# Cumulated gates carried by the scores' second matmul, causal mask read by VectorE from one constant tile

## The chip, the cores and the metric

The kernel runs on one core of a Trainium2 chip. The metric is device time in microseconds (us) of one execution. The engines of a core are PE (TensorE, matrix products), DVE (VectorE), ACT (ScalarE), POOL (GpSimd) and SP (SyncE, which here only issues DMAs). Each engine works through its own instruction list in order, and they meet at semaphores.

## What is computed

One decoder layer on a sequence of 1024 positions of width 1024, in float32. Two groups of heads read the same modulated input; eight of them are the forgetting-attention ("fox") heads that this change is about:

```python
cum = cumsum(log_f)                        # one running sum per head, over the positions
s = einsum('qd,kd->qk', q, k) * scale      # head width 64, scale 1/8
s = s + cum[q] - cum[k]
s = where(key_pos <= q_pos, s, -inf)       # causal mask
p = softmax(s); out = p @ v
```

`cum[q]` is the same for a whole row of scores, so the softmax doesn't see it and the kernel leaves it out. Around the fox heads stand a conditioning row, an input projection, four retention heads, an output projection with a norm, and a gated MLP with a width-3 convolution and a second norm.

## The kernel before

Matrices are split into a high part in fp32r and the rest (`whi`/`wlo`, `hhi`/`hlo`), and a product is made of three matmuls. The program has two parts. A first block `r` (input modulation, retention heads, and the projection `vp` of the fox values and gates) is ordered by a scheduler's simulation. The rest follows it: attention, output projection, MLP.

*Start.* SP loads the conditioning vector `cs` and its bias `bcol`, then, for each of eight slices j of the model width, two slices of modulation weights (`ada`), one of input weights (`wrr`) and one of the transposed input (`xt`). DVE makes scale and shift from `ada`, ACT makes `hhi` from `xt`, and PE runs 21 matmuls per slice (`fa`, `fb`). Before that PE runs matmuls on a tile `warm` of ones.

*End of block r.* `v_proj(c, n)` runs 24 matmuls for each of 16 steps q. `log_forget` makes the log gates `L`, `cum_forget` sums them on PE (`pcum`), `cum_store` turns the result (`pcumT`), copies it (`cumT`) and stores it in DRAM as `cum_d`.

*Attention.* It runs in 64 steps, eight query blocks i for each of eight heads h. `fox_proj(h, .., t, part)` projects queries and keys of half t of the sequence, in four parts of six matmuls, and in its last part ACT and DVE split the result: `qh` holds the high part of -q/8 twice (rows 0-63 and 64-127), `ql` the low part twice, `ks` the high part of k over its low part. `fox_scores(h, i)` multiplies `qh` by `ks` (L799) and `ql` by `ks` (L800), which adds the four products of the parts; a third matmul (L803) multiplies the bf16 identity `identb` by `maskb` and so adds 1e30 above the diagonal of the last 128 columns. DVE (L805) then adds the tile `nb`, the head's cumulated gates broadcast to 128 rows by a DMA of 512 KB, and takes the row minimum in the same instruction; ACT (L812) takes the exponential, POOL (L816) divides. Three steps later `fox_turn` transposes the block on PE (`pt`, L866), ACT (L874) and DVE (L875) split it, and `fox_pv` multiplies by the values. `fox_w(h)` loads and splits the weights of head h as a whole into a pair of tiles of its own, one head ahead.

*Passengers of the attention stage.* `park_load`, `park_high` (ACT, L1032), `park_low` (DVE) and `park_store` split the output weights in 16 loads that pass through SBUF tiles `park` back into DRAM (`wod`), two or three per head; `park_high` of the first load stands on ACT between the exponentials of steps 1 and 2. `down_base(m)` issues on SP, in step 6 of head m, its share of 44 copies of 256 KB from the down-projection weights into a DRAM tensor `td`, which the MLP reads much later. These copies are kept behind the head's `nb` load:

```python
def fox_alloc(h):
    ...
    pins["nb"] = nc.sync.dma_start(t["nb"], ...)
def down_base(m):
    ...
        with tc.issue_after(pins["nb"].ins):
            nc.sync.dma_start(td[q, k], wdq[t, k][:, n * 512:(n + 1) * 512])
```

`issue_after(x)` gives the instructions inside it a place behind x in the list of x's engine; it reaches only instructions on that engine. Instructions with no such edge and no data to wait for are placed wherever the ordering pass finds room. SP's DMAs report on eight semaphores in turn, and a DMA is issued only when the one that last used its semaphore has landed, so at most eight are under way.

The functions that the change touches, with the profile's line numbers:

Of the kernel before, what the change touches and what calls it, by code (L numbers as in the profile page):

```python
# [31 lines left out]
def kernel(  # L32
# [43 lines left out]
    def f(ap):  # L76
        return ap.bitcast(F32)
# [4 lines left out]
    identb = cp.tile([P, P], BF16, tag="identb", name="identb")  # L82
    nc.vector.tensor_copy(identb, ident)
# [4 lines left out]
    maskb = cp.tile([P, P], BF16, tag="maskb", name="maskb")  # L88
    nc.gpsimd.memset(maskb, 0.0)
    nc.gpsimd.affine_select(  # L90
        out=maskb, in_=maskb, pattern=[[-1, P]], compare_op=ALU.is_ge,
        fill=BIG, base=0, channel_multiplier=1,
    )
# [542 lines left out]
    def fox_w(h):  # L636
        raw = slot("R", [P, ND, P], F32, f"wqkr{h}")
        nc.sync.dma_start(raw, w_qk[h])
        whi = slot("X", [P, ND, P], F32R, f"wqh{h}")
        wlo = slot("X", [P, ND, P], F32R, f"wql{h}")  # L640
        nc.scalar.copy(whi, raw)
        for q in range(2):
            sl = slice(4 * q, 4 * q + 4)
            nc.vector.tensor_tensor(
                out=wlo[:, sl, :], in0=raw[:, sl, :], in1=f(whi[:, sl, :]), op=ALU.subtract
            )
        return whi, wlo
# [4 lines left out]
    cum_d = dp.tile([64, P], F32, tag="cum_d", name="cum_d")  # L652
# [67 lines left out]
    def cum_store(cum):  # L720
        pc = bank("pcumT")
        turn(pc[:64, :P], cum.rearrange("p c h -> p (c h)"), ident)
        cumT = tmp([64, P], F32, "cumT")
        nc.vector.tensor_copy(cumT, pc[:64, :P])
        nc.sync.dma_start(cum_d, cumT)

    for q in range(2 * NT):
# [7 lines left out]
        if q == 3:  # L735
            w = fox_w(0)
        if q == 8:
            Lp = log_forget()
        if q == 14:
            cum = cum_forget(Lp)  # L740
            nw = fox_w(1)
        if q == 15:
            cum_store(cum)
# [5 lines left out]

    def fox_alloc(h):  # L750
        t = {n: slot("X", [P, S], F32R, f"{n}{h}") for n in ("qh", "ql", "ks")}
        t["nb"] = slot("X" if h < 2 else "VM", [P, S], F32, f"nb{h}")
        pins["nb"] = nc.sync.dma_start(t["nb"], bass.AP(
            tensor=cum_d.tensor, offset=cum_d.offset + h * S, ap=[[0, P], [1, S]]))
        return t

    def fox_proj(h, w, T, t, part):
        whi, wlo = w
# [1031 lines left out]
```

## Time and profile before

| | |
|---|---|
| median of 3 runs | 1214.06 us (1213.79 to 1214.09) |
| profiled execution: time / span | 1213.8 us / 1212.1 us |
| granted TensorE clock | 0.998 of full speed |
| PE busy / DVE / ACT / POOL | 1195.2 / 912.2 / 655.7 / 229.6 us |
| attention, first to last score matmul | 280.7 to 473.8 us |
| moved by DMA | 216.57 MB, mean 179 GB/s |

The span is the profile's own time from first to last event; the execution's time is 1.7 us longer. A group row of the profile gives line, engine, operation, output and inputs, count, busy time and the mean of one. Rows of the timeline begin with start and duration. In rows of windows the DMA share is the mean busy share of the 16 DMA engines (it can come out a little above 1), and GB/s is what they moved. "SPq" rows are DMA issues by SP; the time from issue to landing stands in the rows on DMA issues.

### The profile page before, as it was taken

How to read it: one execution, taken by the hardware profiler on the slowest of the kernel's cores; microseconds unless marked ns; L12 is line 12 of the kernel's file. 1: busy time of each engine (PE TensorE's matmuls, PEld its weight loads, DVE VectorE, ACT ScalarE, POOL GpSimd, SP SyncE). 2: the span in 40 equal slices, each digit the busy share in tenths (PEclk: the TensorE clock that was granted, in tenths of full speed). 3: DMA queues.
4: the chain of work that ended last, by engine and by line, in shares of the span. 5: the costliest groups of instructions: out<-in, count | busy, mean ns of one | idle time of the engine just before them, and what ended most of it. 6: DMA issues, size and time to landing. Idle time of an engine off the chain costs nothing.

```text
span 1212.1 us, 17100 instructions
## 1 busy us (share of the span) xinstructions
PE 1195.2 (99%) x5957; PEld 1000.4 (83%) x5957; DVE 912.2 (75%) x1749; ACT 655.7 (54%) x1209; POOL 229.6 (19%) x274
## 2 busy tenths in 40 slices
PE   8999999999999999999999999999999999999997
PEld 6788888997888888888888888888888888888885
DVE  7847657766888888456988778787787875886686
ACT  6635445346777776567754545454454555644452
POOL 0015345012333333000021322211000010000021
PEclk9999999999999999999999999999999999999999
DMA  9524354605474659223268987776554589975741
GB/s 359 227 87 121 134 158 138 202 34 175 160 239 156 191 162 356 94 79 113 87 181 203 205 210 182 176 180 175 155 139 125 145 238 289 326 247 190 263 175 70
DMA packets 94279, 216.57 MB, mean 179 GB/s; under 512 B 10784, under 2 KB 17136, under 8 KB 94192
## 3 DMA queue, kind: packets, MB, share of 16 engines
q1 hardware_dynamic: 81520, 192.40, 45.7%
q0 software_dynamic: 12672, 23.07, 11.9%
q8 instruction: 47, 0.77, 0.3%
q14 instruction: 40, 0.33, 0.1%
HBM read 173.45 MB, written 76.59 MB: 206 GB/s over the span
## 4 chain that ended last, share of the span: by engine, by line
PE 91%; DMA 4%; DVE 2%; ACT 1%; issue 0%; SPq 0%; DVEq 0%
PE rp L152 11%; PE dX L1531 10%; PE dZ L1531 7%; PE uX L1306 7%; PE uX L1307 7%; PE uX L1305 7%; PE uY L1307 5%; PE uY L1306 5%; PE uY L1305 5%; PE vp L152 4%; PE pv L886 3%; DMA ada<-in_ada_dram 3%; PE op L191 2%; PE op L189 2%; PE op L190 2%; PE pt L866 2%
## 5 line engine op out<-in xcount | busy, mean ns | idle before, releaser
L152 PE MATMUL rp<-wr,hhi 128*128 128x512 f32 x400 | 127.9, 401 | 0.0
L1517 DVE TENSOR_TENSOR dl<-dr,dh 128x1024 fp32r<-128x1024 f32 x66 | 80.5, 1238 | 33.8 <-ACT dh L1505 31.5
L816 POOL TENSOR_TENSOR S<-S,dn 128x128 f32<-128x128 f32 (+3 forms) x64 | 74.2, 1166 | 151.3 <-DVE dn L815 112.0
L1505 ACT CAST dh<-dr 128x1024 fp32r<-128x1024 f32 x58 | 59.8, 1051 | 65.6 <-DMA dr<-td 30.3
L1148 POOL DMA_DIRECT2D sd<-gd x22 | 18.1, 823 | 396.9 <-DMA sd<-y 226.2
L152 PEld LDWEIGHTS rp<-wr,hhi 128*128 128x128 f32 x400 | 71.6, 189 | 12.7
L152 PE MATMUL rp<-wr,hlo 128*128 128x512 f32 x200 | 78.6, 393 | 0.0
L1531 PE MATMUL dX<-dl,dh 128*128 128x512 f32 x176 | 68.5, 389 | 0.0
L1531 PE MATMUL dX<-dh,dl 128*128 128x512 f32 x176 | 68.5, 389 | 0.0
L1531 PE MATMUL dX<-dh 128*128 128x512 f32 x176 | 68.5, 389 | 0.0
L1320 ACT COPY u<-uX 128x512 f32<-128x512 f32 x44 | 25.8, 586 | 70.3 <-PE uX L1307 70.3
L812 ACT ACTIVATE S<-S,mn 128x128 f32<-128x128 f32 (+3 forms) x64 | 49.8, 779 | 23.9 <-DVE mn L805 23.7
L152 DVE CUSTOM_DVE_ANT_0 ada<-ada,csb,bcol 128x1024 f32<-128x1024 f32 x46 | 60.1, 1310 | 3.4 <-DMA ada<-in_ada_dram 3.3
L875 DVE TENSOR_TENSOR pt<-pt,pt 128x384 fp32r<-128x384 f32 (+3 forms) x104 | 51.9, 517 | 10.2 <-ACT pt L874 9.8
L874 ACT CAST pt<-pt 128x384 fp32r<-128x384 f32 (+3 forms) x104 | 45.2, 454 | 24.9 <-PE pt L866 23.5
L765 PE MATMUL qk<-hhi,wqh 128*128 128x512 f32 x128 | 54.3, 424 | 1.8 <-DVE ks L777 1.5
L1531 PE MATMUL dZ<-dh 128*128 128x512 f32 x132 | 51.6, 391 | 0.0
L1531 PE MATMUL dZ<-dl,dh 128*128 128x512 f32 x132 | 51.4, 389 | 0.0
L1531 PE MATMUL dZ<-dh,dl 128*128 128x512 f32 x132 | 51.4, 389 | 0.0
L767 PE MATMUL qk<-hhi,wql 128*128 128x512 f32 x128 | 51.0, 399 | 0.0
L766 PE MATMUL qk<-hlo,wqh 128*128 128x512 f32 x128 | 50.9, 397 | 0.0
L189 PE MATMUL op<-wo,mxs 128*128 128x512 f32 x128 | 50.7, 396 | 0.0
(1049 smaller groups left out, 3653.3 us busy)
## 6 DMA issues: line engine op xcount, KB each, us to landing
ada<-in_ada_dram SPq DMA_DIRECT2D x48, 512.0 KB, 3.9
td<-in_w_down_dram SPq DMA_DIRECT2D x44, 256.0 KB, 5.6
wa<-in_w_up_dram SPq DMA_DIRECT2D x22, 512.0 KB, 4.5
wb<-in_w_up_dram SPq DMA_DIRECT2D x22, 512.0 KB, 3.7
gd<-y SPq DMA_DIRECT2D x22, 512.0 KB, 2.7
sd<-y SPq DMA_DIRECT2D x44, 256.0 KB, 3.1
dr<-sd SPq DMA_DIRECT2D x44, 256.0 KB, 4.2
dr<-td SPq DMA_DIRECT2D x44, 256.0 KB, 4.4
```

Of the source, the lines that this page charges most:

```text
L152: order[key] = fn(*args, **kw)
L189: mm(pt, ahi, whi, start=start, stop=False)
L765: nc.tensor.matmul(pt, whi[:, j, :], hhi[j][:, sl], start=(j == 0), stop=False)
L767: nc.tensor.matmul(pt, wlo[:, j, :], hhi[j][:, sl], start=False, stop=(j == ND - 1))
L816: nc.gpsimd.tensor_tensor(out=Ssb[:, :span], in0=Ssb[:, :span], in1=den.to_broadcast([P, span]), op=ALU.mult,)
L875: nc.vector.tensor_tensor(out=dl, in0=src, in1=f(dh), op=ALU.subtract)
L1305: nc.tensor.matmul(pt, whi, bh, start=start, stop=False, skip_group_check=True)
L1306: nc.tensor.matmul(pt, whi, bl, start=False, stop=False, skip_group_check=True)
L1307: nc.tensor.matmul(pt, wlo, bh, start=False, stop=stop, skip_group_check=True)
L1505: nc.scalar.copy(hi, raw)
L1517: nc.vector.tensor_tensor(out=lo, in0=raw, in1=f(hi), op=ALU.subtract)
L1531: nc.tensor.matmul(pt, w_[:, 0, q], m_[:, 1, :], start=start and n_ == 0, stop=stop and n_ == 2, skip_group_check=True)
```

## The change

- The mask's matmul, its identity and its tile go. A constant tile `late` [128, 1024] (zeros, and 1e30 above the diagonal in its last 128 columns) takes the place of `nb` as DVE's second operand in the row minimum.
- The cumulated gates enter through the second score matmul. `cum_store` splits them into three fp32r parts and stores them as `cum_d` [3, 64, 128]. Per head a DMA on POOL's queue puts three rows of 4 KB into rows 64-66 of a tile `kc`, under the low part of k, and two constant tiles `q1` carry ones in these rows under the high part of q. The first product is now `qq` (high over low q) by `kk` (high k twice), the second `q1` by `kc` with 67 rows.
- `fox_w` works in halves into one pair of tiles for all heads, at steps 1 and 3 of the head before; the load `fox_load` stands at step 4, one head earlier. `cum_forget` and `cum_store` stand two steps of q earlier.
- `pins["nb"]` is now the `kc` DMA on POOL, so `down_base` names an instruction of POOL's list while its copies are on SP's.

```diff
@@ -79,18 +79,10 @@
 
     ident = cp.tile([P, P], F32, tag="ident", name="ident")
     make_identity(nc, ident)
-    identb = cp.tile([P, P], BF16, tag="identb", name="identb")
-    nc.vector.tensor_copy(identb, ident)
     epsc = cp.tile([P, 1], F32, tag="epsc", name="epsc")
     nc.vector.memset(epsc, LN_EPS)
     ones = cp.tile([P, P], F32, tag="ones", name="ones")
     nc.vector.memset(ones, 1.0)
-    maskb = cp.tile([P, P], BF16, tag="maskb", name="maskb")
-    nc.gpsimd.memset(maskb, 0.0)
-    nc.gpsimd.affine_select(
-        out=maskb, in_=maskb, pattern=[[-1, P]], compare_op=ALU.is_ge,
-        fill=BIG, base=0, channel_multiplier=1,
-    )
     tri = cp.tile([P, P], F32, tag="tri", name="tri")
     nc.gpsimd.memset(tri, 1.0)
     nc.gpsimd.affine_select(
@@ -633,23 +625,24 @@
             v_load(2 * (c - 2))
 
 
-    def fox_w(h):
-        raw = slot("R", [P, ND, P], F32, f"wqkr{h}")
-        nc.sync.dma_start(raw, w_qk[h])
-        whi = slot("X", [P, ND, P], F32R, f"wqh{h}")
-        wlo = slot("X", [P, ND, P], F32R, f"wql{h}")
-        nc.scalar.copy(whi, raw)
-        for q in range(2):
-            sl = slice(4 * q, 4 * q + 4)
-            nc.vector.tensor_tensor(
-                out=wlo[:, sl, :], in0=raw[:, sl, :], in1=f(whi[:, sl, :]), op=ALU.subtract
-            )
-        return whi, wlo
+    wraw = {}
+
+    def fox_load(h):
+        wraw[h] = slot("R", [P, ND, P], F32, f"wqkr{h}")
+        nc.sync.dma_start(wraw[h], w_qk[h])
+
+    def fox_w(h, half):
+        sl = slice(4 * half, 4 * half + 4)
+        raw, (whi, wlo) = wraw[h], wqk
+        nc.scalar.copy(whi[:, sl, :], raw[:, sl, :])
+        nc.vector.tensor_tensor(
+            out=wlo[:, sl, :], in0=raw[:, sl, :], in1=f(whi[:, sl, :]), op=ALU.subtract
+        )
 
 
     L = cp.tile([P, NT, FH], F32, tag="L", name="L")
     V2 = [slot("VM", [P, NT, P], F32R, f"V2_{h}") for h in range(FH)]
-    cum_d = dp.tile([64, P], F32, tag="cum_d", name="cum_d")
+    cum_d = dp.tile([3, 64, P], F32, tag="cum_d", name="cum_d")
 
     def v_proj(c, n):
         n0, n1 = (0, 256) if n == 0 else (256, 520)
@@ -720,9 +713,15 @@
     def cum_store(cum):
         pc = bank("pcumT")
         turn(pc[:64, :P], cum.rearrange("p c h -> p (c h)"), ident)
-        cumT = tmp([64, P], F32, "cumT")
-        nc.vector.tensor_copy(cumT, pc[:64, :P])
-        nc.sync.dma_start(cum_d, cumT)
+        parts = tmp([64, 3 * P], F32R, "cumT").rearrange("h (u q) -> h u q", u=3)
+        rest = tmp([64, P], F32, "cumr")
+        nc.vector.tensor_copy(parts[:, 0, :], pc[:64, :P])
+        nc.vector.tensor_tensor(out=rest, in0=pc[:64, :P], in1=f(parts[:, 0, :]),
+                                op=ALU.subtract)
+        nc.vector.tensor_copy(parts[:, 1, :], rest)
+        nc.vector.tensor_tensor(out=parts[:, 2, :], in0=rest, in1=f(parts[:, 1, :]),
+                                op=ALU.subtract)
+        nc.sync.dma_start(cum_d.rearrange("u h q -> h u q"), f(parts))
 
     for q in range(2 * NT):
         n, c = 1 - q // NT, q % NT
@@ -733,30 +732,45 @@
         if q in (2, 10):
             mod_rows(q // 8)
         if q == 3:
-            w = fox_w(0)
+            wqk = [slot("X", [P, ND, P], F32R, f"wq{n}") for n in "hl"]
+            fox_load(0)
+            for half in range(2):
+                fox_w(0, half)
         if q == 8:
             Lp = log_forget()
+        if q == 12:
+            cum = cum_forget(Lp)
+        if q == 13:
+            cum_store(cum)
         if q == 14:
-            cum = cum_forget(Lp)
-            nw = fox_w(1)
-        if q == 15:
-            cum_store(cum)
+            fox_load(1)
 
     blk.__exit__(None, None, None)
 
     mixF = {}
     pins = {}
 
+    late = slot("X", [P, S], F32, "late")
+    nc.gpsimd.memset(late, 0.0)
+    nc.gpsimd.affine_select(
+        out=late[:, S - P:], in_=late[:, S - P:], pattern=[[-1, P]], compare_op=ALU.is_ge,
+        fill=BIG, base=0, channel_multiplier=1,
+    )
+    q1s = [slot("X", [P, S], F32R, f"q1_{p}") for p in range(2)]
+    NC = 64 + 3
+    for q1 in q1s:
+        nc.gpsimd.memset(f(q1[64:NC, :]), 1.0)
+
     def fox_alloc(h):
-        t = {n: slot("X", [P, S], F32R, f"{n}{h}") for n in ("qh", "ql", "ks")}
-        t["nb"] = slot("X" if h < 2 else "VM", [P, S], F32, f"nb{h}")
-        pins["nb"] = nc.sync.dma_start(t["nb"], bass.AP(
-            tensor=cum_d.tensor, offset=cum_d.offset + h * S, ap=[[0, P], [1, S]]))
+        t = {"qq": slot("X", [P, S], F32R, f"qq{h}"), "kk": slot("X", [P, S], F32R, f"kk{h}"),
+             "kc": slot("X" if h < 2 else "VM", [P, S], F32R, f"kc{h}"), "q1": q1s[h % 2]}
+        pins["nb"] = nc.gpsimd.dma_start(
+            t["kc"][64:NC, :].rearrange("u (c q) -> u c q", q=P), cum_d[:, h * NT:h * NT + NT, :])
         return t
 
-    def fox_proj(h, w, T, t, part):
-        whi, wlo = w
-        qh, ql, ks = T["qh"], T["ql"], T["ks"]
+    def fox_proj(h, T, t, part):
+        whi, wlo = wqk
+        qq, q1, kk, kc = T["qq"], T["q1"], T["kk"], T["kc"]
         sl = slice(t * 512, (t + 1) * 512)
         if part == 0:
             T["pt"] = bank(f"qk{h}_{t}")
@@ -768,20 +782,20 @@
                 pt, wlo[:, j, :], hhi[j][:, sl], start=False, stop=(j == ND - 1)
             )
         if part == 3:
-            nc.scalar.activation(qh[:64, sl], pt[:64], AF.Copy, scale=-0.125)
-            nc.scalar.copy(ks[:64, sl], pt[64:])
+            nc.scalar.activation(qq[:64, sl], pt[:64], AF.Copy, scale=-0.125)
+            nc.scalar.copy(kk[:64, sl], pt[64:])
             nc.vector.scalar_tensor_tensor(
-                out=ql[:64, sl], in0=pt[:64], scalar=-0.125, in1=f(qh[:64, sl]),
+                out=qq[64:, sl], in0=pt[:64], scalar=-0.125, in1=f(qq[:64, sl]),
                 op0=ALU.mult, op1=ALU.subtract,
             )
             nc.vector.tensor_tensor(
-                out=ks[64:, sl], in0=pt[64:], in1=f(ks[:64, sl]), op=ALU.subtract
+                out=kc[:64, sl], in0=pt[64:], in1=f(kk[:64, sl]), op=ALU.subtract
             )
-            nc.scalar.copy(qh[64:, sl], f(qh[:64, sl]))
-            nc.vector.tensor_copy(ql[64:, sl], f(ql[:64, sl]))
+            nc.scalar.copy(q1[:64, sl], f(qq[:64, sl]))
+            nc.vector.tensor_copy(kk[64:, sl], f(kk[:64, sl]))
 
     def fox_scores(h, i, T, beside=None):
-        qh, ql, ks, nb = T["qh"], T["ql"], T["ks"], T["nb"]
+        qq, q1, kk, kc = T["qq"], T["q1"], T["kk"], T["kc"]
         span = (i + 1) * P
         tag = "S" if i % 2 == 0 else "R" if h < FH - 1 else "VM"
         Ssb = slot(tag, [P, S], F32, f"S{h}_{i}")
@@ -795,15 +809,10 @@
         qs = slice(i * P, (i + 1) * P)
         pt = bank2(f"ps{h}_{i}")[:, off:]
         for k0, k1 in cuts:
-            last = k0 <= i * P < k1
-            nc.tensor.matmul(pt[:, k0:k1], qh[:, qs], ks[:, k0:k1], start=True, stop=False)
-            nc.tensor.matmul(pt[:, k0:k1], ql[:, qs], ks[:, k0:k1],
-                             start=False, stop=not last)
-            if last:
-                nc.tensor.matmul(pt[:, i * P:(i + 1) * P], identb, maskb,
-                                 start=False, stop=True)
+            nc.tensor.matmul(pt[:, k0:k1], qq[:, qs], kk[:, k0:k1], start=True, stop=False)
+            nc.tensor.matmul(pt[:, k0:k1], q1[:NC, qs], kc[:NC, k0:k1], start=False, stop=True)
         pins["min"] = nc.vector.tensor_tensor_reduce(
-            out=Ssb[:, :span], in0=pt[:, :span], in1=nb[:, :span], scale=1.0, scalar=3e38,
+            out=Ssb[:, :span], in0=pt[:, :span], in1=late[:, S - span:], scale=1.0, scalar=3e38,
             op0=ALU.add, op1=ALU.min, accum_out=mn,
         )
         if beside is not None:
@@ -1160,15 +1169,15 @@
     LOADS = {0: (4, 5), 1: (6, 7), 2: (0, 1), 3: (2, 3)}
     T = {0: fox_alloc(0)}
     for part in range(4):
-        fox_proj(0, w, T[0], 0, part)
-    fox_proj(0, w, T[0], 1, 0)
+        fox_proj(0, T[0], 0, part)
+    fox_proj(0, T[0], 1, 0)
     Sb = {}
 
     def proj(h, i):
         if i < 3:
-            fox_proj(h, w, T[h], 1, i + 1)
+            fox_proj(h, T[h], 1, i + 1)
         elif h + 1 < FH:
-            fox_proj(h + 1, w, T[h + 1], *divmod(i - 3, 4))
+            fox_proj(h + 1, T[h + 1], *divmod(i - 3, 4))
 
     for s_ in range(FH * NT + LAG + 1):
         h, i = divmod(s_, NT)
@@ -1178,7 +1187,6 @@
                     for half in range(2):
                         mixF[h // 4, half] = slot("VM", [P, 2, 512], F32, f"mixF{h // 4}_{half}")
             if i == 3:
-                w = nw
                 if h + 1 < FH:
                     T[h + 1] = fox_alloc(h + 1)
             if i >= 3:
@@ -1186,7 +1194,7 @@
             k = LOWS.get(s_)
             Sb[s_] = fox_scores(h, i, T[h], None if k is None else lambda: park_low(k))
             if i == 4 and h + 2 < FH:
-                nw = fox_w(h + 2)
+                fox_load(h + 2)
             if i == 6:
                 down_base(h)
             if k is not None:
@@ -1205,6 +1213,8 @@
             fox_turn(r // NT, r % NT, Sb.pop(r))
         if h < FH and not (i >= 3):
             proj(h, i)
+        if i in (1, 3) and h + 1 < FH:
+            fox_w(h + 1, i // 2)
         if h == FH - 1 and i == 0:
             for q in range(2):
                 op_load(q)
```

How the lists of instructions change, at the places that the prediction speaks of.

SP at the start of the program, before (`cs`, `bcol`: conditioning; `ada`, `wrr`, `xt`: the loads of slices 0 and 1):

```order
L102 DMA cs<-in_cT_dram 128x8
L104 DMA bcol<-in_b_cols_dram 128x48
L745 UNCONDITIONAL_BRANCH
L154 DMA ada_0_0_112<-in_ada_dram 128x1024
L152 DMA ada_0_1_113<-in_ada_dram 128x1024
L152 DMA wrr_0_116<-in_w_ret_dram 128x512
```

The same place after the change:

```order
L94 DMA cs<-in_cT_dram 128x8
L96 DMA bcol<-in_b_cols_dram 128x48
L1163 DMA td<-in_w_down_dram 128x512 x9
L748 UNCONDITIONAL_BRANCH
L146 DMA ada_0_0_105<-in_ada_dram 128x1024
L144 DMA ada_0_1_106<-in_ada_dram 128x1024
L144 DMA wrr_0_109<-in_w_ret_dram 128x512
```

Nine of the 44 `td` copies now stand ahead of the first `ada` load.

SP from the store of the cumulated gates into the attention stage, before (`wqkr`: weights of head 2):

```order
L725 DMA cum_d<-cumT 64x128
L745 UNCONDITIONAL_BRANCH
L753 DMA nb_3146<-cum_d 128x1024
L1028 DMA park_1_3200<-in_w_out_dram 128x512
L753 DMA nb_3255<-cum_d 128x1024
L1154 DMA td<-in_w_down_dram 128x512 x3
L1028 DMA park_1_3221<-in_w_out_dram 128x512
L1045 DMA wod_3137<-park_0_3199 128x512
L1154 DMA td<-in_w_down_dram 128x512 x3
L638 DMA wqkr_3306<-in_w_qk_dram 128x1024
```

After the change:

```order
L724 DMA cum_d<-cumT 64x3x128
L748 UNCONDITIONAL_BRANCH
L1163 DMA td<-in_w_down_dram 128x512 x35
L1037 DMA park_1_3200<-in_w_out_dram 128x512
L1037 DMA park_1_3220<-in_w_out_dram 128x512
L1054 DMA wod_3139<-park_0_3199 128x512
L632 DMA wqkr_3305<-in_w_qk_dram 128x1024
```

The other 35 copies, which were spread in groups over eight heads, stand in one piece between the store and the first `park` load.

ACT in the first steps of head 0 after the change, with what each instruction waits for (`DMAHW`: a DMA issued by SP):

```order
L821 ACTIVATE S0_0_3189,dn0_0_3195<-S0_0_3189,mn0_0_3190 128x128 [waits DVE_49]
L821 ACTIVATE S0_1_3208,dn0_1_3214<-S0_1_3208,mn0_1_3209 128x256 [waits DVE_49,Pool_49]
L1041 CAST park0_0_3199<-park0_1_3200 128x512 [waits DMAHW6_49,DMAHW2_49]
L821 ACTIVATE S0_2_3230,dn0_2_3236<-S0_2_3230,mn0_2_3231 128x384 [waits DVE_49]
L637 CAST wqh_2579<-wqkr1_3087 128x512 [waits PE_49]
L785 ACTIVATE qq0_3145<-qk0_1_3180 64x512 [waits PE_49]
```

The cast of the first `park` load kept its place between the exponentials of steps 1 and 2; behind it stand the split of head 0's second half of queries and keys, which step 4's scores need.

## The prediction

> **What bounds the kernel now.** I read the page's busy times and its chain first, then windows of the stages that the change touches, then the timeline of each engine there.
>
> ```profile
> PE 1195.2 (99%) x5957; PEld 1000.4 (83%) x5957; DVE 912.2 (75%) x1749; ACT 655.7 (54%) x1209; POOL 229.6 (19%) x274
> PE 91%; DMA 4%; DVE 2%; ACT 1%; issue 0%; SPq 0%; DVEq 0%
> 11.00:45.00 34.00, 33.83 (x147) 27.23 (x147) 30.87 (x44) 22.87 (x24) 0.00 (x0) 1.00 1.03 407
> 265.00:270.00 5.00, 5.00 (x44) 5.00 (x44) 1.71 (x8) 1.28 (x7) 0.00 (x0) 1.00 0.01 3
> ```
>
> PE is the bound nearly everywhere, so a matmul removed is time gained, and any wait of PE is time lost. The chain's 4% of DMA lies in one place, the start: in the third row (11 to 45 us; behind PEclk 1.00 stand DMA share and GB/s) the DMA engines are full, 1.03, at 407 GB/s, while PE is full too. The last row shows the opposite, the end of block r, where DMA does almost nothing. These two rows decide what the moved `td` copies cost.
>
> ```profile
> 2.19 4.48 DMA ada<-in_ada_dram
> ...
> 34.09 8.98 DMA wrr<-in_w_ret_dram
> ...
> 44.24 1.15 ACT hhi L152
> ...
> 45.43 1.21 PE fa L152 x4
> ```
>
> This is the chain of work from the start: load after load, up to the eighth slice's weights, then ACT, then PE. Every microsecond put ahead of these loads reaches PE at 45.43.
>
> **1. The mask's matmul goes: a gain of 6.2 us.**
>
> ```profile
> L803 PE MATMUL ps<-maskb,identb 128*128 128x128 bf16 x64 | 14.7, 230 | 0.0
> 408.70 0.33 PE L800 MATMUL ps<-ks,ql 128*128 128x384 f32 x1
> 408.88 0.23 PE L803 MATMUL ps<-maskb,identb 128*128 128x128 bf16 x1
> 408.92 0.47 PE L765 MATMUL qk<-hhi,wqh 128*128 128x512 f32 x1
> 409.23 0.40 PE L766 MATMUL qk<-hlo,wqh 128*128 128x512 f32 x1
> ...
> 332.14 0.23 PE L803 MATMUL ps<-maskb,identb 128*128 128x128 bf16 x1
> 332.21 1.05 PE L866 MATMUL pt<-ident,S 128*128 128x128 f32 x8
> ...
> 341.20 0.39 PE L767 MATMUL qk<-hhi,wql 128*128 128x512 f32 x1
> 341.43 0.40 PE L765 MATMUL qk<-hhi,wqh 128*128 128x512 f32 x1
> ```
>
> Matmuls overlap, so the 14.7 us busy are no price; the distance between starts is. From the mask to the next start it is 0.04 us, and that next matmul then holds PE for 0.31 instead of the 0.23 of the last two rows: 0.12 together. Ahead of transposes it is 0.07 and nothing behind. In the timeline 38 of the 64 masks stand ahead of a projection, score or value matmul and 26 ahead of transposes: 38 x 0.12 + 26 x 0.065 = 6.2 us. The ends are 64 x 0.03 = 1.9 (the bare step) and 14.7; I take 6.2, from the starts. Four of the 64 stand ahead of the wait of part 3 and gain nothing: 5.8.
>
> The second product has 67 rows of weights instead of 128 and the same columns; I leave its price as it is (L800's rows show only 128). DVE's minimum reads the same shapes (L805), so it costs the same.
>
> **2. Nine `td` copies ahead of the first load: a loss of 9.0 us, and 1.0 for PE starting again.**
>
> ```profile
> L1154 SPq DMA_DIRECT2D td<-in_w_down_dram x44: 490/594/837, 275.9 to 427.2; - x44
> DMA to landing us min/median/max: 3.2/5.6/7.5
> 408.00:416.00 8.00, 8.00 (x52) 6.62 (x50) 6.73 (x17) 5.30 (x12) 0.83 (x1) 1.00 0.98 312
> 419.00:433.00 14.00, 13.62 (x82) 11.31 (x81) 12.35 (x34) 10.90 (x26) 6.83 (x6) 1.00 0.92 270
> 428.00:430.00 2.00, 2.00 (x14) 1.69 (x13) 2.00 (x7) 1.74 (x4) 0.00 (x0) 1.00 0.92 208
> ...
> 407.72 3.06 SPq L1154 DMA_DIRECT2D td<-in_w_down_dram  x5
> 410.89 0.57 SPq L638 DMA_DIRECT2D wqkr<-in_w_qk_dram  x1
> ...
> 422.98 4.87 SPq L1154 DMA_DIRECT2D td<-in_w_down_dram  x7
> ```
>
> What does a copy of 256 KB from DRAM to DRAM hold the DMA engines for? In 408 to 416 they moved 2.50 MB: five copies (1.31 MB), and about 1.19 MB to or from SBUF, which at the 407 GB/s of the start takes 2.9 us. Of 8 x 0.98 = 7.8 busy us that leaves 4.9 for five, 1.0 us each. In 419 to 433 it is 3.78 MB with ten copies: 12.9 busy minus 1.16 MB at 407 (2.9) leaves 10.0 for ten, again 1.0. The ends: 0.64 us if a copy went at 407 GB/s too, 1.26 at the 208 GB/s of the slowest stretch. I take 1.0, since two stretches agree; SP issues one in 0.59 and is not the limit.
>
> The start has no free DMA time, so nine copies shift its whole stream by 9 x 1.0 = 9.0 us (5.8 to 11.3).
>
> ```profile
> 3.16 1.91 PE L152 MATMUL fb<-warm 128*128 128x512 bf16 x4
> ...
> 7.24 2.10 PE L152 MATMUL fb<-warm 128*128 128x512 bf16 x9
> 10.86 1.21 PE L152 MATMUL fa<-wr,hhi 128*128 128x512 f32 x4 [1.52 <-ACT hhi L152]
> ...
> 45.43 1.21 PE L152 MATMUL fa<-wr,hhi 128*128 128x512 f32 x4 [0.60 <-ACT hhi L152]
> ```
>
> PE has a second loss here. Its first matmuls start 0.43 us apart, the later ones of the same shape 0.21: it runs at half speed from 2.8 to about 7.2 us, and loses 2.2. It then waits from 9.3 to 10.9, and would wait until about 20. Whether a wait of 10 us brings the slow start back no row shows: 0 or 2.2 us. The nearest row is the start itself, so I take 2.2, less the slack at 45.43 and at the first slice, about 1.2: 1.0. [...]
>
> **3. The other 35 copies ahead of the first `park` load: a loss of 23.9 us, and 1.0 for the second restart.** Times here are those of before; the shift of part 2 is added to all alike.
>
> ```profile
> 272.10 0.27 PE L152 MATMUL pcumT<-ident,cum 128*64 128x128 f32 x1
> 272.72 0.53 SPq L725 DMA_DIRECT2D cum_d<-cumT  x1
> 275.02 0.39 SPq L1028 DMA_DIRECT2D park<-in_w_out_dram  x1
> 282.68 0.60 ACT L1032 CAST park<-park 128x512 fp32r<-128x512 f32 x1
> 284.94 0.59 ACT L771 ACTIVATE qh<-qk 64x512 fp32r<-64x512 f32 x1
> 287.50 0.41 DVE L781 CAST ql<-ql 64x512 fp32r<-64x512 f32 x1
> 288.13 0.33 PE L799 MATMUL ps<-ks,qh 128*128 128x384 f32 x1
> L152 PE MATMUL vp<-wv,hhi 128*128 128x264 f32 (+1 forms) x256 | 47.4, 286 | 0.0
> ```
>
> `pcumT` moves forward by 48 `vp` matmuls at 0.12 us, to 266.3. Storing followed it by 0.6; three more small DVE instructions between the evacuations of `vp` add about 1.1: store at 268.0, first copy at 268.7 (its issue takes 0.53 before). The quickest copy landed 3.2 us after its issue, of which 1.0 is moving, so 2.2 are fixed. Then 35 x 1.0, and the `park` load behind them at 0.64 (256 KB at 407 GB/s): it lands at 268.7 + 2.2 + 35.0 + 0.6 = 306.5. ACT wants it at 282.68. Behind it on ACT's list stand the exponential of step 2 and the split of queries and keys (L771 and the next), for which DVE waits (L781), for which PE waits with step 4's scores (288.13). PE has the scores of steps 2 and 3 and some projection to do, until about 288, then nothing. From the cast to those scores it takes ACT and DVE 4.9 us by their durations, and took 5.4 before, so the delay of ACT, 306.5 - 282.7 = 23.8 to 23.9 us, reaches PE whole. By the ends of a copy's price it is 11.3 or 33.0. A second slow start of PE (0 to 2.2) is partly covered, since ACT and DVE have a backlog then: 1.0.
>
> **4. The rest, costed at nothing.** The split of weights in halves (ACT 2 x 0.6 us for 1.05) now stands ahead of the queries' split in step 3, some 1.2 us on ACT and DVE. In head 2 the scores of step 4 came 2.2 us after their inputs (first and second row), which covers it; without that cover it would be up to 0.6 us in each of seven heads, 4 us.
>
> ```profile
> 337.24 0.41 DVE L781 CAST ql<-ql 64x512 fp32r<-64x512 f32 x1
> 339.85 0.33 PE L799 MATMUL ps<-ks,qh 128*128 128x384 f32 x1
> L1148 POOL DMA_DIRECT2D sd<-gd x22 | 18.1, 823 | 396.9 <-DMA sd<-y 226.2
> ```
>
> On POOL, `late`, the rows of ones and two `kc` issues (0.8 us each by the last row) stand ahead of the first division, and a `kc` issue ahead of one division per head. POOL is busy 19%; in head 0 ACT's wait covers it, later the load comes five steps ahead of its use. The weights' single pair makes ACT wait until PE has done with the old half, two steps ahead of the next use. `nb`'s 512 KB per head become 12 KB, in a stage where DMA limits nothing once the copies are through. Preparing `identb` and `maskb` lies ahead of the start's loads.
>
> **Sum**: 1213.8 + 9.0 + 1.0 + 23.9 + 1.0 - 5.8 = 1242.9 us against the profiled execution's own 1213.8, which is 0.26 under the median of 1214.06. I predict 1243, slower by 2.4%.
>
> **Rivals.**
>
> - *The copies go as fast as loads do*, 0.64 us each. For it: parts of the rows above reach 407 GB/s; against it: two stretches give 1.0. Then 5.8 + 1.0 + 11.3 + 1.0 - 5.8 = 13.3, 1227 us. [...] Chance 0.13.
> - *They go slower in a long row*, 1.26: 11.3 + 1.0 + 33.0 + 1.0 - 5.8 = 40.5, 1254 us. For it the 208 GB/s row. Chance 0.15.
> - *The start hides its nine*, if loads behind them overtake: 1233 us. Against it the full DMA engines until 45 us, by which bytes count and not their order. Chance 0.06.
> - *The other side: both groups run in DMA time that is free anyway*, and only the mask's gain is left: 1213.8 - 6.2 = 1207.6 us. It decides at two points: slices must arrive at the start while nine copies are still to come, and the 35 must be through by 282, that is at 0.3 us each. For it, only the idle 265 to 270. Chance 0.05.
> - *The case of the sum*, between 0.85 and 1.15 us a copy: chance 0.61.
>
> **How the numbers follow.** The time is that of the likeliest case, 1243. The range goes from the fast copies, without restarts and with the whole mask (1213.8 + 5.8 + 11.3 - 6.2 = 1225), to the slow ones with both restarts whole (1213.8 + 11.3 + 33.0 + 4.4 - 5.8 = 1257). A change within 0.2% is about what measuring can't tell from none. Faster by more than that holds the fifth case, 0.05; within it I leave 0.02 for copies that cost just what the mask gives; slower is 0.93.
>
> **What would show it.** In the changed kernel's trace: nine L1163 issues ahead of the first `ada` issue, and PE's first `fa` near 20 us instead of 10.9; a row of ACT with the `park` cast idle for over 20 us on a DMA, near 316 us (306.5 plus part 2); PE idle for about as long, from some 298 to 321; L803 gone, with 0.23 us between starts where it stood; PE's matmuls half as fast for some us behind both waits; the rest of the kernel shifted and alike. I am wrong if `ada` loads start near 2 us all the same, if the `park` load lands ahead of ACT, or if a copy takes another time than 1.0 us in a row of 35.

## The result, and the profile after

The changed kernel takes 1243.03 us (median of 4 runs, 1242.73 to 1243.47) against 1214.07 (4 runs, 1213.79 to 1214.24) of the kernel before on the same chip: a ratio of 1.0237, with a 95% interval of 1.0225 to 1.025. It is slower by 29.0 us, and the forecast was 1243.0. The total came out; several of its terms did not, and their errors cancelled. The profiled execution has a span of 1241.0 us, 28.9 more than before.

The page of the changed kernel, its busy times, its chain and the largest new idle time in its groups:

```profile
PE 1193.7 (96%) x5893; PEld 1003.5 (81%) x5893; DVE 915.5 (74%) x1751; ACT 655.4 (53%) x1217; POOL 239.3 (19%) x284
PE 85%; DVE 5%; DMA 4%; ACT 2%; issue 2%; SPq 1%; DVEq 0%; ACTq 0%
L812 PE MATMUL ps<-kk,qq 128*128 128x512 f32 (+2 forms) x96 | 35.6, 372 | 18.0 <-DVE qq L787 17.2 <-DVE kk L795 0.5 <-DVE mn L814 0.3
```

PE was the chain for 91% of the time and is so for 85%: DVE has 5%, SP's queue 1%. The scores' first matmul (L812) alone stands idle for 18.0 us, 17.2 of it in one wait. From the list of PE's waits (us in total, times, the longest):

```profile
PE ps L812 <- DVE qq L787: 17.2, 1, 17.2
PE fa L144 <- ACT hhi L144: 11.3, 1, 11.3
PE qk L779 <- DVE kc L791: 4.3, 7, 0.6
...
PE ps L813 <- DMA kc<-cum_d: 1.3, 1, 1.3
...
PE dX L1541 <- DVE ds L1693: 0.8, 1, 0.8
```

The first two were forecast, the other three were not. Where the two large ones come from stands in the timeline of SP's queue (issue times, not landings):

```profile
1.74 5.71 SPq L1163 DMA_DIRECT2D td<-in_w_down_dram  x9
7.50 0.59 SPq L146 DMA_DIRECT2D ada<-in_ada_dram  x1
...
278.51 29.13 SPq L1163 DMA_DIRECT2D td<-in_w_down_dram  x35
307.73 1.50 SPq L1037 DMA_DIRECT2D park<-in_w_out_dram  x2
```

Nine copies stand ahead of the first `ada` load and 35 ahead of the first `park` load. What waits for those loads is seen on ACT (first row), and behind it on PE (the other two fences, PE's timeline at the start and in head 0):

```profile
314.53 0.62 ACT L1041 CAST park<-park 128x512 fp32r<-128x512 f32 x1 [19.99 <-DMA park<-in_w_out_dram]
```

```profile
20.59 2.07 PE L144 MATMUL fa<-wr,hhi 128*128 128x512 f32 x4 [11.35 <-ACT hhi L144]
22.46 1.36 PE L144 MATMUL fb<-wr,hhi 128*128 128x512 f32 x3
23.65 1.08 PE L144 MATMUL fa<-wr,hhi 128*128 128x512 f32 x4
```

```profile
318.26 0.69 PE L812 MATMUL ps<-kk,qq 128*128 128x384 f32 x1 [17.20 <-DVE qq L787]
318.75 0.52 PE L813 MATMUL ps<-kc,q 67*128 67x384 f32 x1
```

PE's first `fa` starts at 20.59 instead of 10.86, the scores of step 4 at 318.26. Behind both waits PE runs slowly: the seven matmuls from 20.59 take 3.06 us, where full speed needs 1.6 (0.23 each); L812's first row takes 0.69 us, where the same row behind a short wait took 0.45 at full clock (the run with 80 spare matmuls below). The windows of the changed kernel show the granted clock (the number ahead of DMA share and GB/s):

```profile
10.00:15.00 5.00, 0.00 (x0) 0.00 (x0) 0.00 (x0) 0.00 (x0) 0.00 (x0) 0.83 0.92 271
15.00:20.00 5.00, 0.00 (x0) 0.00 (x0) 3.17 (x9) 0.90 (x2) 0.00 (x0) 0.50 1.04 414
20.00:25.00 5.00, 4.41 (x13) 3.57 (x14) 4.40 (x7) 3.91 (x5) 0.00 (x0) 0.65 1.03 406
...
305.00:310.00 5.00, 0.00 (x0) 0.00 (x0) 0.00 (x0) 0.00 (x0) 0.00 (x0) 0.50 1.00 227
...
320.00:325.00 5.00, 5.00 (x19) 4.14 (x19) 2.81 (x9) 2.81 (x7) 1.04 (x1) 0.61 0.47 161
```

The clock falls to 0.50 within each wait and is 0.65 and 0.61 in the slice of five microseconds behind it. During the copies alone (305 to 310) the DMA engines are full at 227 GB/s, during the loads of the start (15 to 20) at 414.

Where the 28.9 us of the spans lie, read from the starts of the same matmul in both traces: +10.0 at the first `qk` matmul; +20.5 more at the second score matmul of step 4 in head 0 (318.75 against 288.30: 30.45); +2.9 more by the start of head 1 (33.3); then heads 1 to 7 give back 5.4 (27.9); the last projection loses 1.0 (28.9).

### The profile page after: what moved, and what is told of

The parts are those of the page before. It is cut to its first block, busy times and chain, and to the rows that moved or that the text cites. A ratio compares the mean times of both kernels' runs of the same rounds, so it can differ in the third digit from the quotient of the medians.

```text
span 1241.0 us, 17008 instructions
## 1 busy us (share of the span) xinstructions
PE 1193.7 (96%) x5893; PEld 1003.5 (81%) x5893; DVE 915.5 (74%) x1751; ACT 655.4 (53%) x1217; POOL 239.3 (19%) x284
## 4 chain that ended last, share of the span: by engine, by line
PE 85%; DVE 5%; DMA 4%; ACT 2%; issue 2%; SPq 1%; DVEq 0%; ACTq 0%
PE rp L144 11%; PE dX L1541 7%; PE uX L1316 6%; PE uX L1317 6%; PE uX L1315 6%; PE dZ L1541 5%; PE uY L1315 5%; PE uY L1317 5%; PE uY L1316 5%; PE vp L144 3%; PE op L183 2%; PE op L182 2%; PE op L181 2%; PE pv L895 2%; PE pt L875 2%; PE fa L144 2%
## 5 line engine op out<-in xcount | busy, mean ns | idle before, releaser
L814 DVE CUSTOM_DVE_ANT_0 S<-ps,late 128x128 f32<-128x128 f32 (+3 forms) x64 | 47.9, 749 | 8.1 <-PE ps L813 7.6
L812 PE MATMUL ps<-kk,qq 128*128 128x512 f32 (+2 forms) x96 | 35.6, 372 | 18.0 <-DVE qq L787 17.2
L781 PE MATMUL qk<-hhi,wql 128*128 128x512 f32 x128 | 52.0, 406 | 0.0
```

The source lines that it names most:

```text
L781: nc.tensor.matmul(pt, wlo[:, j, :], hhi[j][:, sl], start=False, stop=(j == ND - 1))
```

## The experiments

**The copies held back.** `down_base` hangs its 44 copies on `pins["nb"]`, which the change moved from SP's queue to POOL's; the copies stay on SP. Here they hang on an SP DMA again:

```diff
+    pins = {}
...
-        nc.sync.dma_start(wraw[h], w_qk[h])
+        pins["load"] = nc.sync.dma_start(wraw[h], w_qk[h])
...
-            with tc.issue_after(pins["nb"].ins):
+            with tc.issue_after(pins["load"].ins):
```

> The changed kernel, with the td copies kept behind the wqkr load of head h+2, an instruction of SP's own list; they are spread over the heads again. Theory A (the whole loss is the order of the copies: 10.0 us at the start, about 24 in head 0, against a gain of 6.2 on PE): about 1208 us, 5 to 7 us faster than before. Theory B (part of the loss is the new attention itself: kc through POOL's queue, the weights split in halves ahead of the queries): at or above 1214. Under A, L813's wait on the kc load (1.3 us in the changed kernel) shrinks too, since no row of copies fills the DMA engines then.

Measured: 1209.38 us (5 runs), ratio 0.9963 [0.9951, 0.9976], 33.7 less than the changed kernel and 4.9 less than before, just short of the expected 5 to 7. So the copies' place, and with it the edge's engine, is the whole loss; without it the change is a gain. Of the five waits shown above the two long ones and the one for `kc`'s DMA are gone. The one in the last projection stays (1.2 us here), and this one:

```profile
PE qk L779 <- DVE kc L791: 4.1, 7, 0.6
```

**Nine of 44 copies free.** The kernel above, with the first nine copies without an edge, as the changed kernel has them at the start:

```diff
-            with tc.issue_after(pins["load"].ins):
+            pins["n"] = pins.get("n", 0) + 1
+            with ExitStack() as behind:
+                if pins["n"] > 9:
+                    behind.enter_context(tc.issue_after(pins["load"].ins))
```

> As e1_pinned, but the first nine copies free, so that they stand ahead of the first ada load again; the other 35 stay spread. Theory A: e1_pinned plus 10.0 us (nine copies at 0.9 to 1.0 us and about 1.4 us for PE at half clock), about 1218. Rival: the nine are hidden in part and the start's loss needs the rest of the change: plus 0 to 5 us.

Measured: 1219.67 us (4 runs), ratio 1.0045 [1.0031, 1.0058]: 10.3 more than the pinned kernel. The other 35 then cost 1243.0 - 1219.7 = 23.4 us, without the restart's rest and the mask's gain being told apart.

**The copies alone, in the kernel before.** Only the edge is taken away:

```diff
-            with tc.issue_after(pins["nb"].ins):
-                nc.sync.dma_start(td[q, k], ...)
+            nc.sync.dma_start(td[q, k], ...)
```

> The kernel before with only the edge of the 44 td copies taken away: no other part of the change. The issue order puts nine copies ahead of the first ada load and 35 behind the store of cum_d, ahead of nb of head 0 and of the first park load. Theory: the copies' place alone makes the loss, at 0.95 to 1.0 us a copy. Start +10.2; nb lands at 273.3 + 2.2 + 35 x 0.95 to 1.0 + 1.3 = 310 to 312 instead of before 281.4, where the first minimum needs it: 28.6 to 30.6, PE's restart 2 to 2.5: 1214.1 + 41 to 43 = 1255 to 1257.5, ratio about 1.034 to 1.036. Rival: the loss comes from the rest of the change (weights' split, order of steps), and the copies ahead cost half of that or less: under 1235.

Measured: 1256.18 us (4 runs), ratio 1.0344 [1.033, 1.0359], inside the theory's 1255 to 1257.5. In its list of waits PE waits where the theory has it, for the first row minimum, which needs `nb` of head 0 behind 35 copies, and at the start:

```profile
PE ps L799 <- DVE mn L805: 28.7, 2, 28.5
PE fa L152 <- ACT hhi L152: 11.2, 1, 11.2
```

The rest of the change is not needed for the loss. This kernel loses 13 us more than the changed one: its shift grows by 29.0 at step 2's scores in head 0, where the changed kernel has grown by 20.5 at step 4's, and it has no mask's gain to give back.

**`park` taken off the early steps.** The changed kernel with the steps at which parts of `w_out` are split (`park`) taken out of head 0 and added to later heads:

```diff
-    LOWS = [NT * h + i for h in range(FH - 1) for i in ((0, 3, 5) if h in (3, 5) else (3, 5))]
+    LOWS = [NT * h + i for h in range(1, FH - 1) for i in ((5,) if h == 1 else (0, 3, 5))]
```

> The changed kernel with all 44 copies where it has them, but the sixteen park loads taken by later steps (none in head 0, one in head 1, three each in heads 2 to 6). Theory A (head 0 loses its time only because ACT stands on the first park load behind 35 copies): about 1220 us (1218 to 1224), that is 20 to 24 less than the changed kernel; the 10 us of the start, the kc wait and some half clock stay. Rival C (35 copies in a row slow the stage by contention whatever waits for a load): above 1235.

Measured: 1225.04 us (4 runs), ratio 1.0096 [1.0079, 1.0112]: 18.0 less than the changed kernel, 2 below the expected 20 to 24. The long wait of head 0 is gone, as it should be if it is ACT's wait for `park`; the list of PE's waits shows what took its place:

```profile
PE fa L144 <- ACT hhi L144: 12.4, 1, 12.4
...
PE pt L875 <- DVE pt L884: 2.2, 2, 2.0
```

The wait at the start was 1 us longer in this execution, and one of 2.0 us came in head 1 (319.8). ACT's timeline has the reason for that one: the load that stood next behind the 35 copies was now the one of head 2's weights (`wqkr`, issued at 310.08), ACT stands idle for it for 3.08 us until 316.94, and the exponential behind it, the division and PE's transposition come late. So the 35 copies still cost something there, by another load.

**PE kept busy at the start.** 46 more spare matmuls ahead of the first `fa`:

```diff
-    keep_on(9)
+    keep_on(55)
```

> The changed kernel with 46 more matmuls on the tile warm ahead of PE's first real one, so that PE works through its wait of 11.4 us at the start. Theory A (the wait itself brings the clock to half, which costs 1.4 us after it): 1241.5 us, 1.2 to 1.7 less than the changed kernel, and the granted clock stays at 1.00 up to 25 us. Rival: the slow restart is hidden behind the loads: no change.

Measured: 1241.43 us (4 runs), ratio 1.0225 [1.0211, 1.0239], 1.6 less by the medians, while the intervals of the two ratios overlap. The clock is 1.00 in the slice that had 0.65 (and in the one ahead of it, which had 0.50):

```profile
20.00:25.00 5.00, 4.08 (x16) 3.04 (x17) 4.37 (x7) 3.90 (x5) 0.00 (x0) 1.00 1.03 407
```

**PE kept busy in head 0's wait.** The changed kernel with spare matmuls ahead of step 4's scores:

```diff
-            nc.tensor.matmul(
+            pins["pj"] = nc.tensor.matmul(                 # in fox_proj
...
+            if s_ == 4:
+                spare = bank("spare")
+                with tc.issue_after(pins["pj"].ins):
+                    for _ in range(70):
+                        pins["sp"] = nc.tensor.matmul(spare, hhi[0][:, :P],
+                                                      hhi[1][:, :512], start=True, stop=True)
-            Sb[s_] = fox_scores(...)
+            with tc.issue_after(pins["sp"].ins) if s_ == 4 else nullcontext():
+                Sb[s_] = fox_scores(...)
```

> The changed kernel with 70 spare matmuls of 128x512 (0.227 us each at full clock, 15.9 us) on PE between the projection and the scores of step 4 in head 0, inside the wait of 17.2 us for the first park load; nothing reads their result. They should end about 1.3 us before those scores can start. Theory: the restart behind that wait, at half clock for some 6.5 us, cost 2.4 to 2.9 us; without it the time is 1243.0 - 2.4 to 2.9 = 1240.1 to 1240.6. Rival, the sum's own term: the restart costs 1.0 us since ACT and DVE are behind anyway: 1242. If the spare matmuls don't hold the clock, or a half clock at their beginning makes them outlast the wait: 1243 or more.

Measured: 1242.38 us (4 runs), ratio 1.0231 [1.0217, 1.0245]. By the number alone the rival with its 1.0 us would have won. The trace says otherwise: the slow clock was not taken away. PE's timeline and a window:

```profile
300.21 16.03 PE L1199 MATMUL spare<-hhi,hhi 128*128 128x512 f32 x70
318.68 0.45 PE L812 MATMUL ps<-kk,qq 128*128 128x384 f32 x1 [2.45 <-DVE qq L787]
```

```profile
320.00:325.00 5.00, 5.00 (x20) 4.26 (x21) 3.44 (x10) 2.91 (x7) 2.30 (x2) 0.67 0.43 157
```

A wait of 2.45 us was left, and the clock was 0.67 behind it. So the run told nothing of the restart's price, and was made again with 80:

```diff
-                    for _ in range(70):
+                    for _ in range(80):
```

> As e6_warm_park, with 80 spare matmuls instead of 70. There the 70 ended 2.45 us before step 4's scores could start, and the granted clock fell to 0.67 in 320 to 325 us behind that short wait all the same; 80 end 18.2 us after 300.2, 0.2 us before the scores can start. Theory: the clock stays at 1.00, and the 2.3 us that PE lost between step 4's scores and the end of head 0 (shift 30.66 to 32.98) do not come: 1239.7 to 1240.5. Rival, the sum's own reason for 1.0: ACT and DVE are behind by then and PE waits for them instead: 1241.5 to 1242.5. In the trace the matmuls behind the wait stand 0.23 us apart instead of 0.43, and the waits on DVE grow or don't.

Measured: 1240.22 us (4 runs), ratio 1.0214 [1.02, 1.0228], 2.8 less than the changed kernel. The wait left is 0.37 us and the clock stays at 1.00:

```profile
317.47 0.45 PE L812 MATMUL ps<-kk,qq 128*128 128x384 f32 x1 [0.37 <-DVE qq L787]
```

```profile
320.00:325.00 5.00, 4.53 (x24) 3.65 (x23) 4.27 (x13) 4.00 (x11) 2.56 (x3) 1.00 0.47 160
```

PE's shift to the kernel before is 25.6 at the end of attention instead of 27.9. So 2.3 of the 3.4 us between the two profiled executions (spans of 1241.0 and 1237.6) lie there; the rest is the late wait for L1693, which this execution does not have.

**The mask's matmul alone, taken out of the kernel before** (which then leaves out the causal mask):

```diff
-            nc.tensor.matmul(pt[:, k0:k1], ql[:, qs], ks[:, k0:k1], start=False, stop=not last)
-            if last:
-                nc.tensor.matmul(pt[:, i * P:(i + 1) * P], identb, maskb, start=False, stop=True)
+            nc.tensor.matmul(pt[:, k0:k1], ql[:, qs], ks[:, k0:k1], start=False, stop=True)
```

> The kernel before without the mask's matmul: the causal mask is left out, nothing else is changed. Theory: the mask's matmul is worth 6.2 us by the starts of the matmuls, and what the pinned kernel misses of it (4.9 measured) is lost to waits on DVE that the changed order brings: 1214.1 - 5.5 to 6.2 = 1207.9 to 1208.6, ratio 0.9949 to 0.9955. Rival: the waits on DVE at step 7 come whenever PE is faster, whatever the order, and take 2.6 us back here too: 1210 to 1211.

Measured: 1212.27 us (11 runs), ratio 0.9985 [0.9976, 0.9993]: 1.9 us, not 5.5 to 6.2; even the rival's 1210 is missed.

**The mask's matmul put back into the pinned kernel**, with its identity and its tile:

```diff
...
-            nc.tensor.matmul(pt[:, k0:k1], q1[:NC, qs], kc[:NC, k0:k1], start=False, stop=True)
+            last = k0 <= i * P < k1
+            nc.tensor.matmul(pt[:, k0:k1], q1[:NC, qs], kc[:NC, k0:k1], start=False, stop=not last)
+            if last:
+                nc.tensor.matmul(pt[:, i * P:(i + 1) * P], identb, maskb, start=False, stop=True)
```

> The pinned kernel with the mask's matmul put back behind the second score matmul (the minimum still adds the constant tile; the mask is added twice). PE's order there changes between kinds of matmul (projection, scores, transposes, values) as often as in the pinned kernel: 258 times against 260. Theory: a mask matmul costs 0.075 to 0.09 us of PE's running time, 4.8 to 5.6 in 64, but makes the waits on DVE shorter by as much as they grew when it was taken out of the kernel before (2.3 to 5.8 us of waits there, 3.5): 1209.4 + 1.3 to 2.1 = 1210.7 to 1211.5. Then taking it out is worth about 2 us in both orders, and the rest of the pinned kernel's 4.9 comes from PE's order (260 changes instead of 275, 0.08 us each, 1.2 us) and other matmuls of the values in one row. Rival, the sum's own term: 6.2 us come back, 1215.6.

Measured: 1214.25 us (11 runs), ratio 1.0 [0.9991, 1.0009]: 4.9 more than without it. Neither value came: the theory of 2 us in both orders falls, and the sum's 6.2 is 1.3 too high.

**The new wait on DVE taken away.** The pinned kernel, with the minimum of step 6 behind the subtraction that PE waits for:

```diff
-            nc.vector.tensor_tensor(
+            pins["kc"] = nc.vector.tensor_tensor(          # the subtraction, in fox_proj
...
+        behind = i == 6 and h + 1 < FH
+        with tc.issue_after(pins["kc"].ins) if behind else nullcontext():
-        pins["min"] = nc.vector.tensor_tensor_reduce(...)
+            pins["min"] = nc.vector.tensor_tensor_reduce(...)
```

> The pinned kernel with one more edge: in step 6 of each head DVE subtracts the keys' rest (kc) ahead of the row minimum, not behind it. In the pinned kernel PE waits for that subtraction seven times by 0.4 to 0.6 us, 4.1 us in all, where the kernel before has four waits of 0.4 (1.5 in all): 2.6 us more. Theory: this wait takes the rest of the mask's gain in attention; with kc 1.1 us earlier it goes, the shift at the end of attention is -8 instead of -4 us, and the time falls by 2.5 to 4 us below the pinned kernel's 1209.4: 1205.4 to 1207, a ratio of 0.993 to 0.994 to before. Rival 1: the minimum of step 6, now 1.3 us later, holds its pair of banks or the exponential longer, and PE waits there by as much: 1209 to 1210. Rival 2: the gain arrives in attention but the last projection is bound by DVE and its loads, so the end shows only part of it: 1207.5 to 1209.

Measured: 1210.88 us (9 runs), ratio 0.9974 [0.9964, 0.9984]: 1.5 more than the pinned kernel's median (the intervals of the ratios overlap), where 2.5 to 4 less were expected. The seven waits did go, 4.1 us, and 2.1 came in their place on `pt`; and still attention became longer, by 1.9 us in the windows below. Rival 1's 1209 to 1210 is the nearest and is missed by 0.9; its mechanism, longer waits of PE elsewhere, does not show in PE's idle time, which is shorter (2.8 us against 4.9; below stands what that time leaves out). (The profiled executions have nearly one span, 1209.1 and 1209.5, as the pinned one also has a wait of 1.2 us in the last projection.)

**What the last three share** is seen in one window of each trace, from the first `qk` matmul to the last of `op`, the same work on PE in all but the mask (us of the window, then PE's busy time and its matmuls). In this order: before; before without the mask; pinned; pinned with the mask; pinned with `kc` first.

```profile
272.13:571.67 299.54, 296.63 (x1642) 247.94 (x1640) 219.69 (x594) 207.42 (x477) 74.16 (x64) 1.00 0.52 174
```

```profile
272.53:570.66 298.13, 291.94 (x1578) 245.81 (x1576) 221.37 (x594) 207.93 (x477) 74.11 (x64) 1.00 0.52 175
```

```profile
273.20:567.60 294.40, 289.47 (x1578) 246.92 (x1577) 225.16 (x596) 207.02 (x485) 83.06 (x75) 1.00 0.48 162
```

```profile
272.33:571.96 299.63, 295.31 (x1642) 248.48 (x1641) 227.54 (x595) 207.06 (x485) 83.21 (x75) 1.00 0.48 159
```

```profile
272.41:568.67 296.26, 293.46 (x1578) 246.38 (x1576) 229.17 (x595) 206.68 (x485) 82.92 (x75) 1.00 0.48 161
```

Window minus busy time is PE's idle time: 2.9, 6.2, 4.9, 4.3 and 2.8 us. By these records the mask's 64 matmuls are worth 4.7 us of PE's busy time in the old order, and 3.3 of it comes back as waits on DVE (for the last reader of a projection's bank 3.7 instead of 1.5, for `pt` ahead of the values 1.7 instead of 0.5). In the new order they are worth 5.8, and 0.6 comes back.

The three kernels without the mask have the same 1578 matmuls and differ by 4.0 us in the time in which PE is busy. That time grows with the number of changes between kinds of matmul in PE's order (projection, scores, transposes, values, `op`): 256 in the pinned kernel, 282 in the kernel before without the mask and 309 with `kc` first, for 289.5, 291.9 and 293.5 us. But the starts do not show a price of a change. The same place at the end of head 1, in the pinned kernel and with `kc` first:

```profile
320.27 0.60 PE L875 MATMUL pt<-ident,S 128*128 128x128 f32 x4
320.63 0.48 PE L812 MATMUL ps<-kk,qq 128*128 128x512 f32 x1
320.94 0.40 PE L813 MATMUL ps<-kc,q 67*128 67x512 f32 x1
321.19 0.40 PE L812 MATMUL ps<-kk,qq 128*128 128x512 f32 x1
321.42 0.40 PE L813 MATMUL ps<-kc,q 67*128 67x512 f32 x1
322.43 0.47 PE L779 MATMUL qk<-hhi,wqh 128*128 128x512 f32 x1 [0.61 <-DVE kc L791]
322.74 0.40 PE L780 MATMUL qk<-hlo,wqh 128*128 128x512 f32 x1
```

```profile
320.85 0.39 PE L813 MATMUL ps<-kc,q 67*128 67x512 f32 x1
321.20 0.47 PE L779 MATMUL qk<-hhi,wqh 128*128 128x512 f32 x1
321.50 0.40 PE L780 MATMUL qk<-hlo,wqh 128*128 128x512 f32 x1
```

Behind the four transpositions L812 holds PE for 0.31 us instead of 0.23, but the four took 0.36 from start to start, where four at 0.11 (the eight in the prediction's rows) take 0.44: in sum this change costs nothing. And busy time is not all work. A matmul's record reaches 0.16 us beyond the start of the next (0.39 against 0.23), so that much of each wait counts as busy, and a shorter wait shows as none. The wait of 0.61 us costs 0.86 in starts, 1.01 and 0.31 where 0.23 each is usual; with `kc` first the same place costs 0.19, 0.35 and 0.30, and no wait is shown. The lengths of the windows are sure, then; their split into work and waits is off by 0.2 to 0.25 us for each wait, and what makes the 4.0 us stays open.

## Why the prediction was right, point by point

**Part 1, the mask, 6.2 or 5.8 net.** In the changed kernel heads 1 to 7 give back 5.4 us, which is 56/64 of 6.2. But the term was read as the worth of an instruction, and it is not one: 1.9 us in the old order, 4.9 in the new. The step that failed stands in the prediction's first paragraph: that PE is the bound, so a matmul removed is time gained. The waits on DVE behind it (L777 in the kernel before, four times up to 0.4) were in the trace and were not priced; without the mask they were seven and 3.7 us.

**Part 2, nine copies, 9.0 and 1.0.** Measured +10.0 at the first `qk` matmul and 10.3 by the run with nine. PE's restart there is worth 1.6 by the medians of the run with spare matmuls and 0.7 by the shift in its trace (9.25), which lacks the late wait for L1693 too; 1.0 lies between. One trace is a rough measure here: in the six with nine copies in front and no spare matmuls at the start the shift at the first `qk` is 10.0 to 12.2. In the changed kernel, with 10.0, the half clock lasts 2.95 us from the first `fa` on (20.59 to 23.54).

**Part 3, 35 copies, 23.9 and 1.0.** The mechanism is as told: ACT idle for the `park` load, PE behind it at step 4's scores. From the first copy's issue to the cast it takes 314.53 - 278.51 = 36.0 us; less 2.2 and 0.64 that is 33.2 for 35 copies, 0.95 each. The cast was forecast at 316.5 and came 2.0 earlier. PE lost 20.5 up to step 4's scores, not 23.9. The other part of the difference is the way from the cast to those scores, 3.73 us (314.53 to 318.26) where the prediction had 4.9 by the durations and 5.4 before: PE waits there for `qq`, the first of DVE's three instructions of the split (L787), where the prediction let it wait for the last (L781). Of the 20.5 the 17.2 us are the wait itself, the rest two short waits (1.3 and 0.35) and the slow clock behind them. The second restart cost 2.3 by the traces and 2.8 by the medians (the run with 80), and not 1.0: the reason given, that ACT and DVE have a backlog, did not hold, since with PE at full clock the waits on them did not take the gain. These are the mis-sized terms: 23.9 was 3.4 too much, 1.0 was 1.9 too little, by the shifts (20.5 and 2.9).

**Part 4, the rest at nothing.** The pinned kernel with the mask put back is the rest of the change without copies and mask: ratio 1.0 [0.9991, 1.0009]. So nothing is right as a net, and wrong in its reason: by the records PE needs 1.3 us less in the new order and waits 1.4 more. The named fallback, 0.6 us in each of seven heads, came, but at another place: PE's wait for the projection's bank at step 7, not for step 4's scores; with the old 1.5 us taken off it is 2.8.

**Not foreseen.** `kc`'s DMA, issued by POOL at 284.68 among the copies, makes PE wait 1.3 us at 292.70; the longer wait that follows covers this. The 1.0 us at the end is a wait of the last projection on DVE (1202.63), which the profiles of some of these kernels have and others not; its cause stays open. The chain's 4% of DMA does not lie at the start alone, as the prediction read it: of the longest pieces of the chain 40.7 us do, and 9.0 lie in attention (`wqkr` at 285.53, `wod` at 314.45); no term hung on this.

**The sum.** 10.0 + 20.5 + 2.9 - 5.4 + 1.0 = 29.0 against 9.0 + 1.0 + 23.9 + 1.0 - 5.8 = 29.1. The agreement to 0.1 us is luck; a copy's price of 0.95 and the chain through `park` are not.

**The rivals.** Copies at 0.64 or 1.26 us: both excluded, by 0.95 in the row of 35. The start hides its nine: excluded, 10.3 us. The other side, copies in free time: excluded by both waits. The pinned kernel at 1209.4 is what that side would have been, and 1.8 us slower than its 1207.6. The restarts stood in the sum with 1.0 each, 2.0 after slack; measured are 0.7 to 1.6 and 2.3 to 2.8.

## What to carry to other kernels

When an instruction moves to another engine's queue, look for what was ordered behind it: an edge that holds on one engine only ceases to hold, and the work that it kept late (here 44 copies of 256 KB) goes to the front of its queue. A matmul taken from a nearly full PE is worth its start-to-start distance only as far as no other engine ends just behind it (here 1.9 and 4.9 us, where the starts gave 6.2); read the short waits of the old trace before crediting it, and remember that a wait hides up to 0.16 us in the record of the matmul before it.

## What the runs showed of the hardware that I had not expected

The granted clock fell after shorter waits than I had reckoned with (the prediction asks it of a wait of 10 us). Behind a wait of 1.29 us (0.35 just before it) PE's matmuls in the changed kernel stand 0.43 us apart, half speed, for some three microseconds (from 293.51 on). The two waits:

```profile
291.05 0.35 PE L812 MATMUL ps<-kk,qq 128*128 128x256 f32 x1 [0.35 <-DVE kk L795]
292.70 0.36 PE L813 MATMUL ps<-kc,q 67*128 67x256 f32 x1 [1.29 <-DMA kc<-cum_d]
```

In the run with 70 spare matmuls waits of 0.35 and 0.48 us at the same place were followed by a clock of 1.00, and 2.45 us later on by 0.67; in the kernel before a wait of 1.52 us at the start (until 10.86) was followed by full speed (1.00 from 11 to 45 us). So in these runs the length of the wait alone does not decide. Two rows of the changed kernel, up to the fall behind the wait of 1.29 us and from it to the way back:

```profile
289.77:293.19 3.42, 1.77 (x10) 1.13 (x9) 1.81 (x3) 0.62 (x1) 0.00 (x0) 1.00 0.95 265
293.19:296.60 3.41, 3.41 (x10) 2.83 (x10) 1.31 (x8) 1.01 (x4) 0.40 (x1) 0.50 1.03 334
```

PE was idle for 1.65 us of the first (3.42 - 1.77, both waits together), and in the second its clock was at half. In the first 330 us of the changed kernel the clock was at half from 13.30 to 23.54, from 293.19 to 296.60 and from 303.43 to 323.91 us. Behind the ends of the two long waits (20.59 and 318.26) that is 2.95 and 5.65 us. No run moved a wait and changed nothing else, so what decides when the clock falls and comes back stays open.

Copies from DRAM to DRAM took 0.95 us per 256 KB in a row of 35, 276 GB/s; in 305 to 310 us it was 227 with the DMA engines full (share 1.00), while the loads of the start had 414 in 15 to 20 us (share 1.04).
